# Latent attention of a two-layer diffusion trunk: value products and modulation steps issued as blocks, softmax normalised on the output

## The chip, the cores and the metric

The kernel runs on one core of a Trainium2 chip. The metric is the device time of one execution in microseconds (us); lower is better. The engines are TensorE (PE, with its weight loads shown apart as PEld), VectorE (DVE), ScalarE (ACT), GpSimd (POOL) and SyncE (SP, which here only issues transfers). About 0.2% (3.7 us here) is what a measurement of this kernel can tell from no change.

## What is computed

Two layers of a trunk over 512 latent and 256 context tokens (width 1024), each with three parallel head groups, an output projection and an MLP. The change is in the latent attention (8 heads, value width 64) and in the modulation vectors:

```
def _modulation(cond, w_mod, b_mod):
    m = jax.nn.silu(cond) @ w_mod + b_mod
    return jnp.split(m[:, None, :], 6, axis=-1)

def block(qi):                       # one block of 128 queries, all 8 heads
    s = jnp.einsum('bhqd,bhkd->bhqk', qi, kall).astype(F32) * scale
    return jnp.einsum('bhqk,bhkd->bhqd', jax.nn.softmax(s, axis=-1).astype(vall.dtype), vall)
```

Latent queries read all 768 keys. Context queries read the 256 context keys, and are needed in layer 0 alone.

## The kernel before

The program is written with tiles and a scheduler: the order in which an engine's instructions are written is a priority, and the scheduler may let a later instruction of an engine pass an earlier one that it holds to be late. Each engine then runs its queue strictly in the order so made.

`mla_attend` works in groups of two heads (`hp`) by 256 queries, and a group has four units (2 heads x 2 blocks of 128 queries). Layer 0 has 12 groups (8 that read 768 keys, 4 that read 256) and 48 units; layer 1 has 8 groups of 768 keys and 32 units. Per unit:

- `scores`: three products in split precision over the keys into a PSUM tile `mm` (L131 to L133; six instructions for 768 keys, three for 256), then `softmax_rows`: the row maximum on DVE (L425, scaled at L427), the exponential with its row sum on ACT (L430, tile `msb`, sum in `msm`), the reciprocal of the sum (L433, `mrc`) and the division of the whole row on DVE (L438).
- two turns later `values`: PE turns the row block by block (L1000, six or two instructions), ACT copies the result to `mpt` (L1001).
- four turns later, once for a group, `output`: 12 (or 4) value products into a PSUM tile `b` (L1013), alternately for head 0 and head 1. Each uses half of the PE array's columns (`tile_position=(0, 64 * z)`), so head 0 and head 1 lie side by side. `split` then writes the high part on ACT (L136) and the low part on DVE (L137).

`heads_in` turns queries and keys of the next two heads (L960). Beside this, layer 0 weaves in two `modulation` vectors: for each of 8 slices of 128 inputs four products that use a quarter of the array's columns each (L150, 32 columns, weights `wm` from memory), and `modulation_rows`, which does the same for a third vector by DVE products (L191). Layer 1 weaves in half of the output projection instead (`out_first`, L1054). After the attention comes the output projection (L1346). Value products and modulation products are plain fp32: one such product is two records in the trace. PSUM gives three buffers to `mm` and two to `b`.

In the trace layer 0's attention lies from about 363.4 us to 510.2 us of the span, layer 1's from 1329.2 us to 1445.7 us.

Of the kernel before, what the change touches and what calls it, by code (L numbers as in the profile page):

```python
# [15 lines left out]
AF = mybir.ActivationFunctionType  # L16
# [8 lines left out]
KD = 8  # L25
# [15 lines left out]
@with_exitstack  # L41
def kernel(ctx, tc, A, dbg=None, stop=None):
    nc = tc.nc
    pe, act, dve, pool, sp = nc.tensor, nc.scalar, nc.vector, nc.gpsimd, nc.sync

    class Stop(Exception):
        pass
# [17 lines left out]
    def psum_banks(mm):  # L65

        ps.stack.close()
        ps.mm, ps.b = mm, 8 - 2 * mm
        ps.n += 1
        ps.pool = ps.stack.enter_context(tc.tile_pool(name=f"ps{ps.n}", bufs=1, space=PSUM, reuse_waits="tile"))  # L70
# [5 lines left out]
    class Pool:  # L76
        def __init__(self, name, side="left"):
            opened.append(self)
            self.st = ExitStack()
            self.p = self.st.enter_context(  # L80
                tc.tile_pool(name=name, bufs=1, side=side, reuse_waits="tile"))
            self.n = 0
# [16 lines left out]
    def b_tile():  # L99
        npsum[0] += 1  # L100
        return ps.pool.tile([128, 512], F32, tag="b", name=f"b{npsum[0]}", bufs=ps.b)

    ident = persist.tile([128, 128], F32, name="ident")
# [8 lines left out]
    qrs = persist.tile([128, 6, 8], F32, name="qrs")  # L112
    cnd = persist.tile([128, KD, 2], F32, name="cnd")
    sp.dma_start(cnd, A["cond"])
    cst = persist.tile([128, KD, 32], F32, name="cst")
# [19 lines left out]
    def split(hi, lo, src):  # L135
        act.activation(hi, src, AF.Copy)  # L136
        dve.tensor_sub(lo, src, r32(hi))  # L137


    def mod_weights(l, v, k, p, bufs):  # L140
        w = p([128, 1024], tag="wm", bufs=bufs)
        sp.dma_start(w, A["w_mod"][l, k * 128:(k + 1) * 128, v * 1024:(v + 1) * 1024])
        return w

    def modulation(l, v, p, bufs=3, ws=None):
        out = b_tile()
        for k in range(KD):
            w = ws[k] if ws else mod_weights(l, v, k, p, bufs)
            for j in range(4):
                pe.matmul(out[32 * j:32 * j + 32, 0:256], cst[:, k, :], w[:, j * 256:(j + 1) * 256],  # L150
                          start=(k == 0), stop=(k == KD - 1), tile_position=(0, 32 * j))
            if k % 2:
                yield
        row = p([128, 256], tag="wr")
        act.activation(row, out[:, 0:256], AF.Copy)
        tr = b_tile()
        for c in range(2):
            pe.transpose(tr[:, c * 128:(c + 1) * 128], row[:, c * 128:(c + 1) * 128], ident)
        trv = tr[:, 0:256].rearrange("p (c j z) -> p j c z", c=2, j=4)
        bm = cols[:, l, C_BMOD + v * 8:C_BMOD + v * 8 + 8].rearrange("p (j c) -> p j c", j=4)  # L160
        for s in range(2):
            dve.tensor_add(mods[:, l, v, :, s].rearrange("p (j c) -> p j c", j=4), trv[:, :, :, s], bm)
        if v % 3 == 1:
            gain(l, v // 3)
        yield
# [252 lines left out]
                                    w[:, :, off:off + 32].rearrange("p r (g c) -> p g r c", g=4))  # L418
        return nb

    def softmax_rows(p, sb, n, nh, tag, scale=None, src=None):

        src = sb if src is None else src
        mx = p([128, nh], tag=tag + "mx", bufs=3)
        dve.tensor_reduce(mx, src, AX.X, ALU.max, negate=True)  # L425
        if scale is not None:
            dve.tensor_mul(mx, mx, scale)  # L427
        sm = p([128, nh], tag=tag + "sm", bufs=3)
        for h in range(nh):
            act.activation(sb[:, h, :n], src[:, h, :n], AF.Exp, bias=mx[:, h:h + 1], scale=1.0 if scale is None else scale[:, h:h + 1],  # L430
                           accum_out=sm[:, h:h + 1])
        rc = p([128, nh], tag=tag + "rc", bufs=3)
        dve.reciprocal(rc, sm)  # L433
        for h in range(nh):
            if h % 2:
                act.activation(sb[:, h, :n], sb[:, h, :n], AF.Copy, scale=rc[:, h:h + 1])
            else:
                dve.tensor_scalar(sb[:, h, :n], sb[:, h, :n], rc[:, h:h + 1], None, ALU.mult)  # L438
# [496 lines left out]
    def mla_attend(l, qrs, qk0, qkd, vd, mh, ml, p):  # L935
# [5 lines left out]
        v = load(p, None, [128, 6, 512], vd)  # L941
# [29 lines left out]
        groups = [(hp, q0, kr_) for hp in range(4)  # L971
                  for q0, kr_ in ((0, full), (256, full)) + (() if last else ((512, ctx_only),))]
        units = [(g, hh, qt) for g in range(len(groups)) for hh in range(2) for qt in range(2)]
        PT, SB = {}, {}

        def scores(u):
            g, hh, qt = units[u]
            hp, q0, kr_ = groups[g]
            qq, kk = T[2 * hp + hh]
            k0 = kr_[0][0]  # L980
            t = mm_tile()
            qs = slice(q0 + qt * 128, q0 + (qt + 1) * 128)
            for a, b in kr_:
                mm3(t[:, a - k0:b - k0], [x[:, qs] for x in qq], [x[:, a:b] for x in kk], True, True)
            nk = NT - k0
            SB[u] = p([128, 1, NT], tag="msb", bufs=MB)
            i, h = q0 // 128 + qt, 2 * hp + hh
            softmax_rows(p, SB[u], nk, 1, "m", qrs[:, i, h:h + 1], t[:, :nk].unsqueeze(1))

        def values(u):  # L990
            g, hh, qt = units[u]
# [12 lines left out]
        def output(u):  # L1004
            g, hh, qt = units[u]
            hp, q0, kr_ = groups[g]
            k0 = kr_[0][0]
            nkt = (NT - k0) // 128
            o = b_tile()
            for c in range(nkt):  # L1010
                for z in range(2):
                    h = 2 * hp + z
                    pe.matmul(o[64 * z:64 * z + 64, 0:256], v[:, k0 // 128 + c, h * 64:(h + 1) * 64],  # L1013
                              PT[g, z][:, c, :], start=(c == 0), stop=(c == nkt - 1), tile_position=(0, 64 * z))
            split(mh[:, hp, q0:q0 + 256], ml[:, hp, q0:q0 + 256], o[:, 0:256])

        n = len(units)
        per = n // 4
# [3 lines left out]
        for u in range(n + LO):  # L1022
# [6 lines left out]
            hp, w = divmod(u, per)  # L1029
# [157 lines left out]
    rb = next(rstd)  # L1187
    wmp.close()
    hp_ = Pool("h0")
    hh, hl = hp_([128, KD, NT], F32R), hp_([128, KD, NT], F32R)  # L1190
# [11 lines left out]
    for l in range(DEPTH):  # L1202
# [4 lines left out]
        if l:  # L1207
            fill = iter(())
            hp_ = Pool(f"h{l}")
            hh, hl = hp_([128, KD, NT], F32R), hp_([128, KD, NT], F32R)  # L1210
# [6 lines left out]
        if l:  # L1217
            squares, sums = mla_in(l, uh, ul, cqh, cql, ssq, sc, fill, late)
# [81 lines left out]
        mh2, ml2 = m2([128, 4, nt], F32R), m2([128, 4, nt], F32R)  # L1300
        sc = Pool(f"ma{l}")
        psum_banks(3)
        if last:
            xp = Pool(f"x{l + 1}", "right")
            xT, acc = xp([128, KD, nt]), xp([128, nt])
            sp.dma_start(xT, xd)
            weave((mla_attend(l, qrs, qk0, qkd[l], vd[l], mh2, ml2, sc), 1.0),
                  (out_first(l, xT, mh, ml, streams), OF))
        else:
            wmp = Pool("wm_rest")  # L1310
            weave((mla_attend(l, qrs, qk0, qkd[l], vd[l], mh2, ml2, sc), 1.0),
                  (chain(*[modulation(0, v, wmp) for v in (2, 4)]), 0.2),
                  (modulation_rows([(0, 3)], cond_rows(wmp), wmp), 0.2))
            wmp.close()
        sc.close()
        tap(f"mixb{l}", mh2); tap(f"mixbl{l}", ml2)
        tap(f"mixa{l}", mh); tap(f"mixal{l}", ml)
# [13 lines left out]
        for m in range(KD):  # L1331
            ks = range(8)
            if last:
# [3 lines left out]
                w = [x[:, m % 2 * 512:] for x in w2]  # L1337
# [200 lines left out]
```

## Time and profile before

| | |
|---|---|
| time, median of 3 runs | 1833.13 us (1832.9 to 1833.24) |
| the profiled execution: time, span | 1833.48 us, 1831.7 us |
| PE busy, of the span | 1752.5 us (96%) |
| DVE busy | 1233.4 us (67%) |
| ACT busy | 754.7 us (41%) |
| mean granted TensorE clock | 0.981 of full speed |

The span is that of the profiled execution, and its time is 1.78 us more. Busy PE counts matmuls whose ends are modelled, and they overlap: how long a piece of work holds PE is read from the start of its first instruction to the start of the next piece.

### The profile page before, as it was taken

How to read it: one execution, taken by the hardware profiler on the slowest of the kernel's cores; microseconds unless marked ns; L12 is line 12 of the kernel's file. 1: busy time of each engine (PE TensorE's matmuls, PEld its weight loads, DVE VectorE, ACT ScalarE, POOL GpSimd, SP SyncE). 2: the span in 40 equal slices, each digit the busy share in tenths (PEclk: the TensorE clock that was granted, in tenths of full speed). 3: DMA queues.
4: the chain of work that ended last, by engine and by line, in shares of the span. 5: the costliest groups of instructions: out<-in, count | busy, mean ns of one | idle time of the engine just before them, and what ended most of it. 6: DMA issues, size and time to landing. Idle time of an engine off the chain costs nothing. (4 is left out here: it accounts for less than half of the span.)

```text
span 1831.7 us, 27057 instructions
## 1 busy us (share of the span) xinstructions
PE 1752.5 (96%) x10794; PEld 1499.4 (82%) x10794; DVE 1233.4 (67%) x2247; ACT 754.7 (41%) x1262; POOL 135.8 (7%) x177
## 2 busy tenths in 40 slices
PE   5999977889999999999999999999999999999999
PEld 2788976756788888888888888888777799999997
DVE  5867777787768877767665447787877665555554
ACT  3624326566734412213212224745666653333331
POOL 1134222200000000000000000231200000000000
PEclk8999989989999999999999999999999999999999
DMA  9225423263153333333332222362041022333232
GB/s 344 72 86 167 148 70 108 82 214 113 53 198 115 138 120 134 117 137 115 130 124 60 67 68 95 114 226 81 24 167 41 31 93 94 97 99 93 93 93 81
DMA packets 73389, 206.11 MB, mean 113 GB/s; under 512 B 12556, under 2 KB 24605, under 8 KB 71856
## 3 DMA queue, kind: packets, MB, share of 16 engines
q1 hardware_dynamic: 71664, 199.15, 32.3%
q0 software_dynamic: 1600, 5.24, 0.8%
q8 instruction: 85, 1.39, 0.3%
q14 instruction: 40, 0.33, 0.1%
HBM read 182.35 MB, written 21.23 MB: 111 GB/s over the span
## 5 line engine op out<-in xcount | busy, mean ns | idle before, releaser
L273 PE MATMUL mm<-t,wh 128*128 128x512 f32 (+1 forms) x2496 | 492.5, 317 | 1.9 <-DVE t L1037 1.3
L136 ACT ACTIVATE wh<-wr 128x1024 fp32r<-128x1024 f32 (+2 forms) x176 | 185.2, 1054 | 599.4 <-PE mm L273 541.4
L273 PEld LDWEIGHTS mm<-t,wh 128*128 128x128 f32 x2496 | 371.4, 189 | 37.9 <-issue 1.9
L273 PE MATMUL mm<-t,wl 128*128 128x512 f32 (+1 forms) x1248 | 296.9, 316 | 0.0
L137 DVE TENSOR_TENSOR wl<-wr,wh 128x1024 fp32r<-128x1024 f32 (+2 forms) x176 | 214.1, 1217 | 30.5 <-ACT wh L136 27.1
L273 PE MATMUL mm<-al,wh 128*128 128x512 f32 (+1 forms) x768 | 233.6, 359 | 0.0
L273 PE MATMUL mm<-ah,wl 128*128 128x512 f32 (+1 forms) x768 | 232.2, 356 | 0.0
L1037 DVE SCALAR_TENSOR_TENSOR t<-mm,mods,t 128x512 f32<-128x512 f32 x216 | 136.3, 659 | 140.6 <-PE mm L273 132.7
L273 PE MATMUL mm<-ah,wh 128*128 128x512 f32 (+1 forms) x768 | 230.9, 354 | 0.0
L273 PEld LDWEIGHTS mm<-t,wl 128*128 128x128 f32 x1248 | 193.6, 189 | 16.2 <-DVE wl L137 0.2
L273 PEld LDWEIGHTS mm<-ah,wl 128*128 128x128 f32 x768 | 127.6, 188 | 22.5
L273 PEld LDWEIGHTS mm<-ah,wh 128*128 128x128 f32 x768 | 126.7, 188 | 23.6
L273 PEld LDWEIGHTS mm<-al,wh 128*128 128x128 f32 x768 | 126.3, 188 | 20.1
L191 DVE SCALAR_TENSOR_TENSOR wmp<-wm,t 128x1024 f32<-128x1024 f32 x64 | 78.3, 1224 | 68.3 <-DMA wm<-in_w_modr_dram 68.3
L425 DVE TENSOR_REDUCE mmx<-mm 128x1 f32<-128x768 f32 (+1 forms) x80 | 67.5, 846 | 24.9 <-PE mm L133 24.2
L136 ACT ACTIVATE ah<-relu 128x768 fp32r<-128x768 f32 (+1 forms) x64 | 47.3, 739 | 87.2 <-DVE relu L1100 87.1
L430 ACT ACTIVATE msb<-mm,mmx,qrs 128x768 f32<-128x768 f32 (+1 forms) x80 | 72.2, 904 | 24.8 <-DVE mmx L427 21.1
L1090 DVE TENSOR_SCALAR bb<-mm,cols 128x2 f32<-128x2 f32 x64 | 14.0, 219 | 97.6 <-PE mm L273 97.4
L191 DVE SCALAR_TENSOR_TENSOR wm<-wm,t 128x1024 f32<-128x1024 f32 x64 | 78.1, 1220 | 0.2
L1001 ACT ACTIVATE mpt<-mm 128x768 f32<-128x768 f32 (+1 forms) x80 | 57.6, 725 | 49.9 <-PE mm L1000 49.8
L137 DVE TENSOR_TENSOR al<-relu,ah 128x768 fp32r<-128x768 f32 (+1 forms) x64 | 52.6, 823 | 36.2 <-ACT ah L136 36.1
L1346 PE MATMUL mm<-t,wh 128*128 128x512 f32 x320 | 76.2, 352 | 0.0
(304 smaller groups left out, 2922.0 us busy)
## 6 DMA issues: line engine op xcount, KB each, us to landing
wr<-in_w_ff_dram SPq DMA_DIRECT2D x128, 512.0 KB, 3.6
wm<-in_w_modr_dram SPq DMA_DIRECT2D x64, 512.0 KB, 4.5
wm<-in_w_mod_dram SPq DMA_DIRECT2D x32, 512.0 KB, 8.4
wr<-in_w_in_t_dram SPq DMA_DIRECT2D x18, 512.0 KB, 4.0
qk<-qk_spill SPq DMA_DIRECT2D x9, 576.0 KB, 5.5
qk_spill<-upk SPq DMA_DIRECT2D x12, 384.0 KB, 2.9
kx<-kk POOLq DMA_DIRECT2D x16, 256.0 KB, 2.5
wr<-in_w_in_qk_dram SPq DMA_DIRECT2D x8, 512.0 KB, 4.6
```

The source lines that it names most:

```text
L136: act.activation(hi, src, AF.Copy)
L137: dve.tensor_sub(lo, src, r32(hi))
L191: dve.scalar_tensor_tensor(w if s else junk, w, 1.0, cr[:, s], ALU.mult, ALU.mult, accum_out=mods[:, l, v, k, s:s + 1])
L273: pe.matmul(out_[:, po:po + b - a], wk[wx], mk[mx][:, a:b], start=(k == 0 and i == 0), stop=(k == nk - 1 and i == 2))
L425: dve.tensor_reduce(mx, src, AX.X, ALU.max, negate=True)
L430: act.activation(sb[:, h, :n], src[:, h, :n], AF.Exp, bias=mx[:, h:h + 1], scale=1.0 if scale is None else scale[:, h:h + 1], accum_out=sm ...
L1001: act.activation(pt[:, 0:nkt, qt * 128:(qt + 1) * 128], tt[:, :nkt * 128].rearrange("p (c q) -> p c q", q=128), AF.Copy)
L1037: dve.scalar_tensor_tensor(xT[:, m, a:b], t[:, a:b], mods[:, l, v, m, s:s + 1], xT[:, m, a:b], ALU.mult, ALU.add)
L1090: dve.tensor_scalar(bb, t[:, 768:770], cols[:, l, C_BF1 + f:C_BF1 + f + 1], None, ALU.add)
L1346: pe.matmul(t[:, a:b], ws[wx], half[mx][:, k % 4, a:b], start=(k == ks[0] and i == 0), stop=(k == 7 and i == 2))
```

## The change

Three things. First, a wrapper round PE's `matmul` and `transpose` that is on in the attention stage alone: matmuls inside a `with pe:` block follow each other on PE with nothing between, everything written before the block stays ahead of it, and everything written after stays behind it. The value products of a group are one such block, and so are the eight modulation products of two slices. Second, the row's division is gone: the sums of a group are kept (`msm`, 2 blocks x 2 heads), and their reciprocal is spread over 128 partitions x 256 (each head's 64 value columns). Third, PE turns that reciprocal (two 128x128 transposes into the unused half of the group's `b` tile), ACT copies it back, and DVE multiplies the group's output by it before `split`.

```diff
+    class Ordered:
+        def after(self, ins, prev):
+            tc.add_manual_dep(ins, prev.name, mybir.DependencyInfo(
+                mybir.DependencyClass.NoSync, mybir.DependencyReason.DATA))
+        def issue(self, r):
+            ins = r.ins
+            if self.on:
+                for prev in self.since if self.inside else []:
+                    self.after(ins, prev)
+                if self.last is not None:
+                    self.after(ins, self.last)
+                if self.inside:
+                    self.since, self.last = [], ins
+                else:
+                    self.since.append(ins)
+            return r
...
     def modulation(l, v, p, bufs=3, ws=None):
-        out = b_tile()
+        out, wk = b_tile(), []
         for k in range(KD):
-            w = ws[k] if ws else mod_weights(l, v, k, p, bufs)
-            for j in range(4):
-                pe.matmul(out[32 * j:32 * j + 32, 0:256], cst[:, k, :], w[:, j * 256:(j + 1) * 256],
-                          start=(k == 0), stop=(k == KD - 1), tile_position=(0, 32 * j))
+            wk.append(ws[k] if ws else mod_weights(l, v, k, p, bufs))
             if k % 2:
+                with pe:
+                    for i in (k - 1, k):
+                        for j in range(4):
+                            pe.matmul(out[32 * j:32 * j + 32, 0:256], cst[:, i, :], wk[i][:, j * 256:(j + 1) * 256],
+                                      start=(i == 0), stop=(i == KD - 1), tile_position=(0, 32 * j))
                 yield
...
-        sm = p([128, nh], tag=tag + "sm", bufs=3)
+        sm = p([128, nh], tag=tag + "sm", bufs=3) if sums is None else sums
         for h in range(nh):
             act.activation(sb[:, h, :n], src[:, h, :n], AF.Exp, ..., accum_out=sm[:, h:h + 1])
+        if sums is not None:
+            return
         rc = p([128, nh], tag=tag + "rc", bufs=3)
...
-            o = b_tile()
-            for c in range(nkt):
-                for z in range(2):
-                    h = 2 * hp + z
-                    pe.matmul(o[64 * z:64 * z + 64, 0:256], v[:, k0 // 128 + c, h * 64:(h + 1) * 64],
-                              PT[g, z][:, c, :], start=(c == 0), stop=(c == nkt - 1), tile_position=(0, 64 * z))
-            split(mh[:, hp, q0:q0 + 256], ml[:, hp, q0:q0 + 256], o[:, 0:256])
+            o, rs = b_tile(), p([128, 2, 128], tag="mrc")
+            rb = rs.rearrange("p t d -> p (t d)")
+            dve.reciprocal(rs.rearrange("p t (z d) -> p t z d", z=2), SM.pop(g).unsqueeze(3).to_broadcast([128, 2, 2, 64]))
+            for t_ in range(2):
+                pe.transpose(o[:, 256 + 128 * t_:384 + 128 * t_], rs[:, t_], ident)
+            act.activation(rb, o[:, 256:512], AF.Copy)
+            with pe:
+                for c in range(nkt):
+                    for z in range(2):
+                        h = 2 * hp + z
+                        pe.matmul(o[64 * z:64 * z + 64, 0:256], v[:, k0 // 128 + c, h * 64:(h + 1) * 64],
+                                  PT[g, z][:, c, :], start=(c == 0), stop=(c == nkt - 1), tile_position=(0, 64 * z))
+            dve.tensor_mul(rb, o[:, 0:256], rb)
+            split(mh[:, hp, q0:q0 + 256], ml[:, hp, q0:q0 + 256], rb)
```

The tile `mrc` has one buffer: it holds the reciprocal, then its turned copy, then the divided output, and the next group's reciprocal is written into it.

The first place is PE's queue in layer 0 of the kernel before, a stretch of some 4 us in the middle of the stage: rows on `b_4117` are value products of one group, `ident,msb` turns a unit's row, and rows on `kh`, `kl` are one unit's scores.

```order
L1013 MATMUL b_4117<-mpt_3970,t_3494 64x256
L1000 MATMUL mm_4093<-ident,msb_4034 128x128 x6
L1013 MATMUL b_4117<-mpt_4043,t_3494 64x256
L1013 MATMUL b_4117<-mpt_3970,t_3494 64x256
L131 MATMUL mm_4101<-kh_3826,qh_3824 128x512
L132 MATMUL mm_4101<-kl_3827,qh_3824 128x512
L133 MATMUL mm_4101<-kh_3826,ql_3825 128x512
L131 MATMUL mm_4101<-kh_3826,qh_3824 128x256
L132 MATMUL mm_4101<-kl_3827,qh_3824 128x256
L133 MATMUL mm_4101<-kh_3826,ql_3825 128x256
L1013 MATMUL b_4117<-mpt_4043,t_3494 64x256
L1000 MATMUL mm_4132<-ident,msb_4059 128x128 x6
```

Value products of one group stand alone or in a few between other work here, and a product for head 1 (`mpt_4043`) is not always next to one for head 0 (`mpt_3970`).

The second place is the same group on PE's queue in the changed kernel (its products are on `b_4060`, after those of the group before, on `b_3964`); L72 and L69 are the wrapper's transpose and matmul, and `mrc` is the reciprocal.

```order
L69 MATMUL b_3964<-mpt_3893,t_3494 64x256
L72 MATMUL mm_3977<-ident,msb_3905 128x128 x6
...
L72 MATMUL mm_3999<-ident,msb_3921 128x128 x6
...
L72 MATMUL mm_4019<-ident,msb_3959 128x128 x6
L72 MATMUL b_4060<-ident,mrc_4061 128x128 x2
...
L69 MATMUL mm_4048<-kh_3795,ql_3794 128x256
L69 MATMUL b_4060<-mpt_3926,t_3494 64x256
L69 MATMUL b_4060<-mpt_3998,t_3494 64x256
L69 MATMUL b_4060<-mpt_3926,t_3494 64x256
```

Between the last product of one group and the two turns of the next group's reciprocal stand three turned rows and (in the left-out lines) two sets of scores; the group's 12 products then follow each other.

The third place is DVE's queue at that same point, before:

```order
L433 RECIPROCAL mrc_3967<-msm_3965 128x1
L427 TENSOR_TENSOR mmx_4004<-mmx_4004,qrs 128x1
L191 SCALAR_TENSOR_TENSOR wm_4152,mods<-wm_4152,t_3488 128x1024
L438 TENSOR_SCALAR msb_3961<-msb_3961,mrc_3967 128x768
L433 RECIPROCAL mrc_4009<-msm_4007 128x1
L425 TENSOR_REDUCE mmx_4035<-mm_4027 128x1
```

and in the changed kernel, where L1067 multiplies a group's output, L176 is the low part of `split`, L1056 the reciprocal, L466 and L468 the row maximum and its scaling, and L232 a modulation product:

```order
L466 TENSOR_REDUCE mmx_3960<-mm_3952 128x1
L468 TENSOR_TENSOR mmx_3960<-mmx_3960,qrs 128x1
L1067 TENSOR_TENSOR mrc_3965<-b_3964,mrc_3965 128x256
L176 TENSOR_TENSOR t_3477<-mrc_3965,t_3476 128x256
L1056 RECIPROCAL mrc_4061<-msm_3880 128x256
L466 TENSOR_REDUCE mmx_3994<-mm_3986 128x1
```

The two instructions for each unit are gone, and the reciprocal of the next group stands right behind the low part of the group before it, whose tile it takes over.

## Rows read from the trace of the kernel before

**Rows 1.** The page's first line.

```profile
span 1831.7 us, 27057 instructions
```

**Rows 2.** Busy time by stretch: us from the start, length, each engine's busy time (instructions).

```profile
core 0: us, PE busy (x) PEld busy (x) DVE busy (x) ACT busy (x) POOL busy (x), PEclk, DMA share, GB/s
...
363.40:437.00 73.60, 64.10 (x419) 45.21 (x420) 59.56 (x134) 47.31 (x81) 0.00 (x0) 0.93 0.53 187
437.00:510.20 73.20, 71.25 (x501) 48.76 (x499) 49.39 (x130) 48.65 (x99) 0.00 (x0) 1.00 0.30 103
510.20:1329.20 819.00, 802.70 (x4728) 703.81 (x4727) 572.77 (x985) 292.88 (x466) 44.37 (x60) 0.99 0.33 112
1329.20:1445.70 116.50, 115.72 (x760) 90.72 (x756) 83.57 (x167) 76.85 (x126) 0.00 (x0) 1.00 0.23 85
```

**Rows 3.** PE's waits in layer 0's attention: in all, times, longest (us).

```profile
PE mm L1000 <- ACT msb L430: 3.9, 1, 3.9
PE mm L1000 <- DVE msb L438: 2.4, 2, 2.1
```

**Rows 4.** PE's timeline in layer 0 (start, us, records): turned row, two products, scores.

```profile
461.26 0.28 PE L133 MATMUL mm<-kh,ql 96*128 96x256 f32 x1
461.39 0.88 PE L1000 MATMUL mm<-ident,msb 128*128 128x128 f32 x6
462.20 0.65 PE L1013 MATMUL b<-mpt,t 128*64 128x256 f32 x4
462.78 0.50 PE L131 MATMUL mm<-kh,qh 96*128 96x512 f32 x1
...
464.03 2.37 PE L1013 MATMUL b<-mpt,t 128*64 128x256 f32 x18
```

**Rows 5.** The same of layer 1: a whole block of 12, one product alone.

```profile
1398.49 0.28 PE L133 MATMUL mm<-kh,ql 96*128 96x256 f32 x1
1398.70 2.81 PE L1013 MATMUL b<-mpt,t 128*64 128x256 f32 x24
1401.45 0.87 PE L1000 MATMUL mm<-ident,msb 128*128 128x128 f32 x6
1402.08 0.71 PE L1054 MATMUL b<-t,wh 128*128 128x512 f32 x2
...
1422.45 0.65 PE L1013 MATMUL b<-mpt,t 128*64 128x256 f32 x2
1423.02 0.50 PE L131 MATMUL mm<-kh,qh 96*128 96x512 f32 x1
...
1439.29 2.18 PE L1000 MATMUL mm<-ident,msb 128*128 128x128 f32 x18
```

**Rows 6.** PE's timeline in layer 0: seven modulation products (14 records).

```profile
500.17 1.06 PE L150 MATMUL b<-wm,cst 128*32 128x256 f32 x14
501.16 0.38 PE L131 MATMUL mm<-kh,qh 96*128 96x256 f32 x1
```

**Rows 7.** DVE's groups by form, layer 0's attention: busy us, mean ns | idle before, releaser.

```profile
L425 DVE TENSOR_REDUCE mmx<-mm 128x1 f32<-128x768 f32 x32 | 30.4, 954 | 13.2 <-PE mm L133 12.9
L438 DVE TENSOR_SCALAR msb<-msb,mrc 128x768 f32<-128x768 f32 x32 | 19.6, 615 | 0.2
...
L433 DVE RECIPROCAL mrc<-msm 128x1 f32<-128x1 f32 x48 | 7.6, 158 | 9.8 <-ACT msb L430 9.3
...
L438 DVE TENSOR_SCALAR msb<-msb,mrc 128x256 f32<-128x256 f32 x16 | 5.5, 351 | 0.2
L137 DVE TENSOR_TENSOR t<-b,t 128x256 fp32r<-128x256 f32 x11 | 4.6, 423 | 3.4 <-ACT t L136 3.3
```

**Rows 8.** Reciprocals of one and two columns: ns min/median/max.

```profile
L433 DVE RECIPROCAL mrc<-msm x80: 150/160/167, 375.0 to 1439.0; 128x1 f32<-128x1 f32 x80
L374 DVE RECIPROCAL rnc<-rnt x6: 166/166/167, 47.3 to 141.8; 128x2 f32<-128x2 f32 x6
```

**Rows 9.** ACT's groups by form, layer 0's attention: copies of 128x256.

```profile
L136 ACT ACTIVATE t<-b 128x256 fp32r<-128x256 f32 x11 | 4.2, 385 | 8.3 <-PE b L1013 8.3
```

More of the change, by code (lines that the diff above doesn't have):

```diff
@@ L43, with __init__, matmul, transpose @@
     nc = tc.nc
-    pe, act, dve, pool, sp = nc.tensor, nc.scalar, nc.vector, nc.gpsimd, nc.sync
+    act, dve, pool, sp = nc.scalar, nc.vector, nc.gpsimd, nc.sync
+    class Ordered:
+        def __init__(self):
+            self.on, self.inside, self.last, self.since = False, False, None, []
+        def after(self, ins, prev):
[13 more added lines that the diff above has]
+            return r
+        def matmul(self, *a, **k):
+            return self.issue(nc.tensor.matmul(*a, **k))
+        def transpose(self, *a, **k):
+            return self.issue(nc.tensor.transpose(*a, **k))
+        def order(self, on):
+            self.on, self.last, self.since = on, None, []
+        def __enter__(self):
+            self.inside = True
+        def __exit__(self, *_):
+            self.inside = False
+    pe = Ordered()
     class Stop(Exception):
@@ L419, in na_bias, with softmax_rows @@
         return nb
-    def softmax_rows(p, sb, n, nh, tag, scale=None, src=None):
+    def softmax_rows(p, sb, n, nh, tag, scale=None, src=None, sums=None):
         src = sb if src is None else src
@@ L973, in mla_attend @@
         units = [(g, hh, qt) for g in range(len(groups)) for hh in range(2) for qt in range(2)]
-        PT, SB = {}, {}
+        PT, SB, SM = {}, {}, {}
         def scores(u):
@@ L978, in scores @@
             hp, q0, kr_ = groups[g]
+            if hh == qt == 0:
+                SM[g] = p([128, 2, 2], tag="msm", bufs=3)
             qq, kk = T[2 * hp + hh]
@@ L987, in scores @@
             i, h = q0 // 128 + qt, 2 * hp + hh
-            softmax_rows(p, SB[u], nk, 1, "m", qrs[:, i, h:h + 1], t[:, :nk].unsqueeze(1))
+            softmax_rows(p, SB[u], nk, 1, "m", qrs[:, i, h:h + 1], t[:, :nk].unsqueeze(1), SM[g][:, qt, hh:hh + 1])
         def values(u):
@@ L1302 @@
         psum_banks(3)
+        pe.order(True)
         if last:
@@ L1314 @@
             wmp.close()
+        pe.order(False)
         sc.close()
```

## Prediction

> **What bounds the kernel now.** I read the page first and then its busy time by stretch. The span is 1831.7 us [rows 1] and the profiled time 1833.48 us, so 1.78 us lie around the span; the median of the runs shown is 1833.13 us, 0.35 us below the profiled run. By stretch [rows 2] PE is busy 64.1 of 73.6 us in the first half of layer 0's attention, 71.25 of 73.2 us in its second half, 115.72 of 116.5 us in layer 1's, and 802.7 of 819 us between the two stages. So from 437 us on PE is what the time follows, and what PE does not have to do there comes off the time. In the first half PE waits: most of it twice, 3.9 us and 2.1 us, for a unit's softmax [rows 3]. DVE is the next engine: 59.56 of 73.6 us in that half, far less elsewhere.
>
> **What a column block costs PE.** The reader should look at starts, not at busy times. One value product alone (2 records) holds PE from 1422.45 to 1423.02, 0.57 us [rows 5]. Two products, one for each head, hold it from 462.20 to 462.78, 0.58 us [rows 4]. A whole block of 12 (24 records) takes 1398.70 to 1401.45, 2.75 us [rows 5]. So the unit is a *pair*: 0.43 us each ((2.75 - 0.58) / 5), plus about 0.15 us once for every run of such products, and a product without its partner costs as much as the pair. Seven modulation products take 500.17 to 501.16, 0.99 us [rows 6]: two sets of four at 0.42 us and the same 0.15 us.
>
> Beside that a run costs something at its edge: from the last score instruction to a turned row 0.13 us pass (461.26 to 461.39 [rows 4]), to a value product 0.21 us (1398.49 to 1398.70 [rows 5]); six turns take 0.63 us when other work follows (1401.45 to 1402.08 [rows 5]) and 0.81 us when products follow (461.39 to 462.20 [rows 4]). So an entry costs 0.08 us after scores, 0.18 us after turns.
>
> **What the blocks save.** I counted runs and pairs in the two built orders.
>
> - Layer 0, value products: 112 products stand in 36 runs that fill 68 pairs; after, 12 runs and 56 pairs. 36 x 0.15 + 68 x 0.43 = 34.6 us become 12 x 0.15 + 56 x 0.43 = 25.9 us: -8.7 us.
> - Layer 0, modulation: 64 products in 19 runs and 21 sets become 8 runs and 16 sets: 19 x 0.15 + 21 x 0.42 = 11.7 us become 7.9 us: -3.8 us.
> - Layer 0, entries: 27 after scores become 8, 14 after turns become 10: 19 x 0.08 + 4 x 0.18 = -2.2 us.
> - Layer 1, value products: 96 products in 14 runs and 53 pairs become 8 runs and 48 pairs: 24.9 us become 21.8 us: -3.1 us; entries after scores 7 to 3: -0.3 us. Layer 1 was nearly blocked before.
>
> **What is added on PE.** Two turns for each group, 24 and 16. Eighteen turns in a row hold PE 2.18 us [rows 5], 0.12 us each: +2.9 us and +1.9 us. PE's sum is -11.8 us in layer 0 and -1.5 us in layer 1, -13.3 us.
>
> **Off PE's path.** In layer 0 DVE loses 19.6 + 5.5 us of divisions and 7.6 us of small reciprocals [rows 7], and gets 12 reciprocals of 128x256 and 12 products of that size out of PSUM; the latter I take like the low part, 0.42 us [rows 7]. No row shows a wide reciprocal. The low bound is a simple operation of that size, 0.35 us (the division of 256 columns [rows 7]). The high bound is the slope of the reciprocals themselves: 160 ns for one column, 166 ns for two [rows 8], some 7 ns (6 to 7) a column, so 0.16 + 255 x 0.007 = 1.94 us. I take 1.9 us, since those rows are the same operation. DVE then changes by 12 x (1.9 + 0.42) - 32.7 = -4.9 us (with the low bound -23.5 us). ACT gets 12 and 8 copies of 128x256 at 0.385 us [rows 9], 7.7 us in all, under 47.31 and 48.65 us of work in halves of 73 us and 76.85 us in 116.5 us [rows 2]: hidden while PE has work in its queue, and behind the chain below where it has not.
>
> The Trainium skill (VectorE: DVE Perf Modes, First, the fixed hardware budget) says that the reciprocal is an iterative divide with a repeat count of 8. With the clock of 0.96 GHz under Specifications there, an estimate for 256 columns is 256 x 8 / 0.96, about 2.1 us. No row of this kernel shows it; with it in place of 1.9 us the chain below is 0.2 us longer in each hand-over between groups, and the sum would be 1 to 2 us worse.
>
> **The first waits.** A row is now turned as soon as its exponential ends: 0.615 + 0.158 = 0.77 us earlier [rows 7]. The two exposed waits of 3.9 and 2.1 us [rows 3] shrink by that each, -1.5 us; what is late next there is the exponential itself. The later waits of layer 0 are short, and layer 1 starts with projection products to fill them; I count nothing there.
>
> **A new chain between groups.** The tile `mrc` has one buffer. So after a group's last product come, in this order, the output's multiplication (0.42 us), the high part on ACT (0.385 us), the low part on DVE (0.42 us), the next group's reciprocal (1.9 us), and only then can PE turn it: 3.1 us plus hand-overs. PE's queue is in order, so if the turns come up earlier, the scores, turned rows and products behind them wait too. How long PE has until then I summed from the new order with the prices above: at the place shown, three turned rows at about 0.6 us and two sets of scores at 1.2 us (462.78 to 464.03 less the entry [rows 4]), 4.2 us. Of 18 hand-overs ten have 4.9 to 13.9 us, and eight (five in layer 0, three in layer 1) have 3.3 to 4.4 us. Those eight have no room for one instruction that stands ahead in DVE's queue (a row maximum takes 0.954 us [rows 7]). The reciprocal also stands ahead of the next row maximum, which then comes 1.9 us later. I charge the eight 0.6 us each: +5 us. Bounds: nothing with the cheap reciprocal; 8 x 1.6 us = 13 us if two such instructions are always ahead.
>
> **The ends.** After the last group the multiplication makes the chain to the output projection 0.42 us longer. The projection takes its input slices in order and needs that group's heads as the last of each, so it starts on work that is ready: hidden, and 0.4 us if not. The modulation weights are now needed for two slices at a time; eight such steps share layer 0's two stretches of 73 us [rows 2], some 18 us for each, in which their transfers land. A late one would hold PE at its block with everything behind it; I count nothing.
>
> **The sum.** -13.3 - 1.5 + 5 = -9.8 us from 1833.48 us gives 1823.7 us for such an execution, 1823.3 us as a median: **1823 us**.
>
> **Rivals.**
>
> *No new wait, 1818 us.* If a wide reciprocal costs like a simple operation (0.35 us), the chain is 1.6 us and all 18 hand-overs have room: -14.8 us from 1833.1 us, 1818 us; a little less if the half-speed stretches at layer 0's start shrink as well (PEclk 0.93 in the first half [rows 2]). For it: 6 ns between two rows of 160 and 166 ns is a thin slope, and the spread of one form is 17 ns. Against: nothing else there names a cheap one. Chance 0.2.
>
> *Layer 0 follows DVE, 1829 us.* In the first half DVE is busy 59.56 of 73.6 us with PE waiting for it [rows 2, 3]. DVE keeps nearly all its work there when the reciprocal is 1.9 us. If that half does not get shorter at all, about half of layer 0's 11.8 us is lost: 1833.1 - 13.3 + 5.9 - 1.5 + 5 = 1829 us. Against: there PE waited for single chains, not for a full queue. Chance 0.2.
>
> *Slower: the hand-overs stall, 1838 us.* The mechanism of the eight tight groups in all 18: the reciprocal waits for the fourth exponential and the tile, DVE's modulation products stand between, and PE stands at two turns with everything behind them. It decides at a stall of 14.8 / 18, about 0.8 us for each group; 1.1 us for each gives 1838 us. Against: ten have room of 4.9 us and more. Chance 0.07.
>
> *The blocks give nothing.* If pairs in one long block cost as much as pairs in short runs, the entries and the 0.15 us of a run stay, and only the missing pairs and sets count, 17 x 0.43 + 5 x 0.42 = 9.4 us against 4.8 us of turns: 1833.1 - 9.4 + 4.8 - 1.5 + 5 = 1832 us. But the whole block of 12 is already in the trace at 2.75 us. Chance 0.03.
>
> **Numbers.** The forecast with its own bounds (stalls of 0 to 9 us) is 1818 to 1828 us, chance 0.5. With the cheap reciprocal below and DVE's pace above, 1815 to 1831 us leaves out the stalled case and the tails. Against a band of 3.7 us (below 1829.4 us is faster, above 1836.8 us is slower): faster 0.49 + 0.2 + 0.1 = 0.79; same 0.14; slower 0.07.
>
> **What would show it.** In the changed profile: value products in 20 groups of 24 or 8 records with 2.74 and 1.01 us from start to next start; a row RECIPROCAL of 128x256 at 1.9 us; 40 more turns; layer 0's stretch about 136.5 us (146.8 - 11.8 - 1.5 + 3), layer 1's about 117 us (116.5 - 1.5 + 1.8); PE waits on `mrc` of about 5 us in all, at the groups with little work between blocks. The prediction is wrong if PE's waits in layer 0 grow by more than 10 us, or if the reciprocal is under 0.5 us and they still grow.

## The result and the profile after

The changed kernel takes 1849.68 us (median of 4 runs, 1843.11 to 1852.97) beside 1833.02 us of the kernel before: ratio 1.0087, interval 1.0063 to 1.011. Run once more in another session, it takes 1846.02 us (8 runs) beside 1837.26 us (25 runs of the kernel before, 1832.72 to 1843.68): 1.0053, interval 1.0033 to 1.0073. It is slower, by 9 to 17 us, where 10 us less was forecast. (A ratio is taken over all runs of both kernels, so it need not be that of the medians.)

The profiled execution takes 1849.73 us with a span of 1848 us, against [rows 1]. Its busy time by stretch (columns as in [rows 2]): up to the attention of layer 0, that attention, the work between, the attention of layer 1.

```profile
0.00:368.10 368.10, 320.58 (x1986) 265.79 (x1986) 256.41 (x541) 161.16 (x335) 91.36 (x117) 0.96 0.38 131
368.10:523.70 155.60, 132.99 (x960) 98.64 (x960) 105.49 (x189) 99.62 (x191) 0.00 (x0) 0.96 0.40 146
523.70:1340.10 816.40, 801.09 (x4710) 702.92 (x4709) 572.90 (x985) 292.69 (x466) 44.29 (x60) 0.99 0.33 111
1340.10:1461.90 121.80, 115.94 (x774) 91.90 (x772) 78.61 (x120) 79.18 (x134) 0.00 (x0) 1.00 0.23 81
```

Layer 0's attention is 155.6 us long with PE busy for 133 us of it: PE stands still for 22.6 us, where it did for 11.4 us before. Layer 1's grew from 116.5 to 121.8 us with PE's busy time almost the same (115.72 and 115.94 us).

One trap is in the first row. The first stage starts at 368.1 us instead of 363.4 us, though PE's order up to there is the same. That part is not the change's: in the 14 profiles of this study (13 kernels, the changed one twice) the first turn of `qk` starts anywhere from 362.7 to 372.2 us. One place where it differs is early: the same modulation records in the kernel before and, in the second pair of rows, in the changed kernel (PE's timeline):

```profile
36.56 1.93 PE L150 MATMUL b<-wm,cst 128*32 128x256 f32 x32
...
39.58 0.64 PE L150 MATMUL b<-wm,cst 128*32 128x256 f32 x8
```
```profile
38.45 3.64 PE L69 MATMUL b<-wm,cst 128*32 128x256 f32 x32
...
43.27 0.64 PE L69 MATMUL b<-wm,cst 128*32 128x256 f32 x8
```

Each of the 32 records takes nearly twice as long in the changed kernel, as at the lower of PE's two clock levels (1.2 for 2.4 GHz); the eight a little later take the same time in both. The granted clock is given as 1.00 for both places, but in the changed kernel that is no reading: its trace has no clock entry before 43.2 us. In the three profiles whose first stage starts latest (368.2, 369.7 and 372.2 us) the first entry, at the upper level, comes at 43.2, 49.4 and 50.6 us; in the other eleven PE is at the upper level from 34.2 to 35.9 us on. So a late rise of the clock goes with a late start; what delays it the runs do not show. Since this lies ahead of all that the change touches, I read each kernel by stage as well: **L0**, from layer 0's first turn of `qk` to one fixed matmul of the output projection behind it (169.2 us before), and **L1**, the same for layer 1, up to one fixed matmul of the work behind its projection (139.4 us). By these the changed kernel loses 5.6 us in L0 and 5.3 us in L1 in the first profile, 4.8 and 5.4 us in the second; the rest of the first run's 16 us is 4.7 us ahead of the stages and 0.7 us between them.

PE's waits in layer 0 and then in layer 1 (in all, times, longest), which answer to [rows 3]:

```profile
PE mm L69 <- ACT mpt L1046: 5.5, 9, 0.9
PE mm L72 <- DVE ql L1007: 5.1, 4, 1.6
PE mm L72 <- ACT msb L471: 4.7, 4, 3.5
PE b L69 <- ACT mrc L1060: 2.7, 4, 0.8
PE mm L69 <- DVE ql L1007: 1.8, 2, 1.1
PE mm L72 <- ACT mpt L1046: 0.7, 3, 0.2
...
PE b L69 <- ACT mrc L1060: 2.9, 4, 1.3
PE mm L69 <- ACT mpt L1046: 1.4, 2, 0.7
```

The largest are waits for a buffer `mm`: scores (L69) that can't start before ACT has copied an earlier turned row out (`mpt`), turns (L72) that can't start before DVE has written the low part of a head (`ql`). The waits of `b` are a group's first product, which waits for ACT's copy of the turned reciprocal.

The same kinds of wait for a buffer `mm` in layer 0 of the kernel before:

```profile
PE mm L1000 <- DVE ql L964: 1.8, 1, 1.8
PE mm L960 <- DVE ql L964: 0.7, 1, 0.7
...
PE mm L960 <- ACT mpt L1001: 0.2, 1, 0.2
```

So the waits for `mpt` rose from 0.2 to 6.2 us and those for `ql` from 2.5 to 6.9 us, while those of a turned row for its softmax fell from 6.3 us ([rows 3]) to 4.7 us.

PE's timeline shows one of each: in layer 0 (first four rows), and in layer 1.

```profile
454.79 0.82 PE L72 MATMUL mm<-ident,msb 128*128 128x128 f32 x6
455.44 0.38 PE L72 MATMUL b<-ident,mrc 128*128 128x128 f32 x2
456.51 0.50 PE L69 MATMUL mm<-kh,qh 96*128 96x512 f32 x1 [0.68 <-ACT mpt L1046]
...
457.75 1.08 PE L69 MATMUL b<-mpt,t 128*64 128x256 f32 x8
...
1380.15 0.38 PE L72 MATMUL b<-ident,mrc 128*128 128x128 f32 x2
1381.07 2.81 PE L69 MATMUL b<-mpt,t 128*64 128x256 f32 x24 [0.53 <-ACT mrc L1060]
1383.81 0.87 PE L72 MATMUL mm<-ident,msb 128*128 128x128 f32 x6
```

Compare [rows 4]: there two value products stand between a turned row and the next scores, and no wait. Here the products of the group whose reciprocal was just turned come as a block only after those scores, and PE waits 0.68 us for the buffer.

DVE's and ACT's new instructions in layer 0, by form (as in [rows 7, 9]):

```profile
L1056 DVE RECIPROCAL mrc<-msm 128x256 f32<-128x256 f32 x12 | 20.9, 1745 | 0.6 <-ACT msb L471 0.5
...
L1067 DVE TENSOR_TENSOR mrc<-b,mrc 128x256 f32<-128x256 f32 x11 | 4.7, 423 | 17.8 <-PE b L69 17.7
```
```profile
L1060 ACT ACTIVATE mrc<-b 128x256 f32<-128x256 f32 x12 | 4.6, 380 | 3.8 <-PE b L72 3.8
```

### The profile page after: what moved, and what is told of

Read it like the earlier page. It is cut to its first block, busy times and chain, and to the rows that moved or that the text cites. A ratio compares the mean times of both kernels' runs of the same rounds, so it can differ in the third digit from the quotient of the medians.

```text
span 1848.0 us, 27007 instructions
## 1 busy us (share of the span) xinstructions
PE 1752.9 (95%) x10834; PEld 1505.5 (81%) x10834; DVE 1225.4 (66%) x2127; ACT 760.5 (41%) x1282; POOL 135.6 (7%) x177
## 5 line engine op out<-in xcount | busy, mean ns | idle before, releaser
L69 PE MATMUL mm<-t,wh 128*128 128x258 f32 (+2 forms) x2816 | 570.0, 322 | 1.8 <-DVE t L176 0.6
L69 PEld LDWEIGHTS mm<-t,wh 128*128 128x128 f32 x2816 | 423.2, 189 | 47.6 <-issue 2.3
L69 PE MATMUL mm<-t,wl 128*128 128x258 f32 (+2 forms) x1408 | 342.7, 320 | 0.0
L69 PEld LDWEIGHTS mm<-t,wl 128*128 128x128 f32 x1408 | 219.0, 189 | 20.4 <-issue 0.4
L69 PE MATMUL mm<-al,wh 128*128 128x512 f32 (+1 forms) x768 | 233.8, 359 | 0.0
L69 PE MATMUL mm<-ah,wl 128*128 128x512 f32 (+1 forms) x768 | 232.4, 356 | 0.0
L176 DVE TENSOR_TENSOR wl<-wr,wh 128x1024 fp32r<-128x1024 f32 (+2 forms) x176 | 213.9, 1216 | 26.9 <-ACT wh L175 23.6
L69 PE MATMUL mm<-ah,wh 128*128 128x512 f32 (+1 forms) x768 | 231.0, 354 | 0.0
L69 PEld LDWEIGHTS mm<-ah,wh 128*128 128x128 f32 x768 | 126.8, 188 | 23.5
L69 PEld LDWEIGHTS mm<-ah,wl 128*128 128x128 f32 x768 | 127.7, 188 | 22.4
L69 PEld LDWEIGHTS mm<-al,wh 128*128 128x128 f32 x768 | 126.3, 188 | 20.0
L232 DVE SCALAR_TENSOR_TENSOR wmp<-wm,t 128x1024 f32<-128x1024 f32 x64 | 78.3, 1223 | 69.4 <-DMA wm<-in_w_modr_dram 67.3
L69 PE MATMUL b<-wh,t 128*128 128x256 f32 (+1 forms) x416 | 94.3, 309 | 4.6 <-ACT hu L658 3.9
L466 DVE TENSOR_REDUCE mmx<-mm 128x1 f32<-128x768 f32 (+1 forms) x80 | 66.8, 841 | 32.4 <-PE mm L69 31.0
L69 PEld LDWEIGHTS b<-wh,t 128*128 128x128 f32 x416 | 73.3, 205 | 6.4 <-ACT hu L658 4.3
L232 DVE SCALAR_TENSOR_TENSOR wm<-wm,t 128x1024 f32<-128x1024 f32 x64 | 78.0, 1218 | 0.1
```

What stands on the lines that cost most here:

```text
L69: return self.issue(nc.tensor.matmul(*a, **k))
L232: dve.scalar_tensor_tensor(w if s else junk, w, 1.0, cr[:, s], ALU.mult, ALU.mult, accum_out=mods[:, l, v, k, s:s + 1])
```

## The experiments

Two words first. A *barrier* is either side of a block: what is written before it stays ahead on PE, what is written after stays behind. *Fill* is small work that PE does while its next larger work waits for something.

Times of one session are read against the kernel before in that session. A difference below 3.7 us cannot be told from no change by the medians; several below are that small, and for those the readings by stage decide. These come from one profile for each kernel; the two profiles of the changed kernel agree within 0.8 us in L0 and 0.1 us in L1 and in idle time. Besides L0 and L1 I worked out from PE's records, between layer 0's first turn and its last value product: how long value and modulation products hold PE (start to next start, less idle time), the same for the turns of the reciprocal, and PE's idle time (end of one record to the start of the next). "Half" is how much of L0 lay at the lower level of PE's clock, 1.2 GHz; each us there costs at most half a us, so kernels that differ in it compare better by idle time than by L0.

| kernel | median, us | before beside it | ratio | L0 | half | products | turns | idle | L1 |
|---|---|---|---|---|---|---|---|---|---|
| before | 1833.0 | | | 169.2 | 10.2 | 46.4 | | 11.4 | 139.4 |
| changed | 1849.7 | 1833.0 | 1.0087 | 174.8 | 13.7 | 36.3 | 4.3 | 22.6 | 144.7 |
| changed, again | 1846.0 | 1837.3 | 1.0053 | 174.0 | 10.2 | 35.1 | 4.3 | 22.5 | 144.8 |
| blocks alone | 1842.7 | 1838.7 | 1.0030 | 174.3 | 17.1 | 38.3 | | 23.9 | 140.9 |
| normalisation alone | 1840.2 | 1838.7 | 1.0016 | 171.2 | 10.2 | 42.3 | 4.1 | 12.0 | 142.7 |
| changed, narrow reciprocal | 1842.2 | 1838.7 | 1.0023 | 172.3 | 13.7 | 35.7 | 4.5 | 21.7 | 144.9 |
| changed, turns into `mm` | 1851.3 | 1838.7 | 1.0073 | 179.7 | 10.2 | 35.7 | 3.9 | 27.5 | 142.4 |
| value blocks alone | 1833.7 | 1837.3 | 0.9983 | 167.5 | 13.7 | 38.8 | | 17.2 | 140.6 |
| modulation blocks alone | 1832.4 | 1837.0 | 0.9975 | 165.6 | 6.8 | 41.7 | | 12.7 | 139.5 |
| blocks in thirds | 1835.4 | 1837.3 | 0.9991 | 163.5 | 6.8 | 36.7 | | 15.2 | 143.4 |
| thirds, modulation free | 1837.9 | 1837.0 | 1.0012 | 167.0 | 13.7 | 40.8 | | 13.9 | 143.2 |
| heads swapped | 1826.7 | 1837.3 | 0.9949 | 162.3 | 10.2 | 38.8 | | 12.7 | 138.1 |
| heads swapped, modulation blocks | 1829.5 | 1837.0 | 0.9966 | 164.3 | 6.8 | 36.9 | | 15.5 | 138.2 |
| heads swapped, normalisation | 1836.0 | 1837.0 | 1.0000 | 167.9 | 10.2 | 40.5 | 4.0 | 10.6 | 141.6 |

**The two halves of the change.** First the blocks with the old softmax:

```diff
-            o, rs = b_tile(), p([128, 2, 128], tag="mrc")
-            dve.reciprocal(...)
-            for t_ in range(2): pe.transpose(...)
-            act.activation(rb, o[:, 256:512], AF.Copy)
+            o = b_tile()
...
-            dve.tensor_mul(rb, o[:, 0:256], rb)
```

> The ordering wrapper and both kinds of block, with the old softmax (reciprocal of each row's sum, rows divided on DVE); nothing is turned, copied or multiplied at a group's end. Theory A (the barriers at both sides of a block take PE's freedom to fill waits): most of layer 0's 11 us of added PE waits stay, mainly scores that wait for ACT's copy to `mpt`, so my PE sum without the turns (-18 us) is largely eaten: 1825 to 1833 us. Theory B (the new chain reciprocal, turn, copy, block is what costs): the added waits go, and the time is near 1833 - 18 = 1815 us, 1812 to 1822 us. Theory C (about 4.7 us of the loss lie ahead of the first attention stage, in code whose order is unchanged, and belong to where the half-clock stretches fall, not to the change): the first stage may begin anywhere from 363 to 368 us here too.

Measured +4.0 us (interval of the ratio 1.001 to 1.0051). The waits stay without any normalisation, as in theory A: 23.9 us idle in layer 0. They eat the whole saving, more than A's 1825 to 1833 us allowed, and they are not the ones that A named: scores wait only 1.2 us for `mpt`, and the largest are those of turned rows for `ql`. As in theory C the start has its part: the first stage begins at 369.7 us, one of the three late ones. PE's waits in layer 0:

```profile
PE mm L72 <- DVE ql L1007: 8.9, 6, 2.1
PE mm L72 <- ACT msb L471: 5.8, 4, 4.5
PE mm L69 <- ACT msb L471: 3.2, 5, 0.9
PE mm L72 <- DVE mmx L468: 2.9, 3, 1.4
PE mm L69 <- ACT mpt L1044: 1.2, 3, 0.5
```

Then the normalisation with no order (the order is never switched on, modulation as before):

```diff
-        pe.order(True)
...
-        pe.order(False)
```

> The other half alone: no ordering and modulation as before; the sums' wide reciprocal, its two turns, the copy and the output's multiplication stay. Theory A: without barriers the scheduler fills the waits, so only the 4.8 us of turns less 1.5 us of the first waits remain: about 1836 us, 1833 to 1839 us. Theory B: PE still waits for the copy before a group's first product and for DVE behind 20 reciprocals of 1.75 us: 1842 to 1850 us.

Measured +1.5 us (1.0004 to 1.0029), and by stage +2.0 and +3.3 us; idle 12.0 us in layer 0, near the kernel before. The 5.3 us of the two stages are nearer to theory A (some 3 us more) than to B (9 us or more). In layer 1 the two halves' costs, +1.5 and +3.3 us, make most of the changed kernel's 5.3 us.

**Two repairs of the chain.** The narrow reciprocal:

```diff
-            dve.reciprocal(rs.rearrange("p t (z d) -> p t z d", z=2), SM.pop(g).unsqueeze(3).to_broadcast([128, 2, 2, 64]))
+            r4 = p([128, 2, 2], tag="mr4", bufs=2)
+            dve.reciprocal(r4, SM.pop(g))
+            dve.tensor_copy(rs.rearrange("p t (z d) -> p t z d", z=2), r4.unsqueeze(3).to_broadcast([128, 2, 2, 64]))
```

> The full change, but the reciprocal is taken of the four sums of a group alone (128x4) and spread to 128x256 by a copy on DVE: about 0.17 + 0.35 us in place of 1.75 us, twenty times. If the wide reciprocal makes DVE late (waits for `ql` of 5.8 us, for row maxima, and the hand-over of the one `mrc` buffer), the time falls by 4 to 10 us from 1849.7 us, to 1840 to 1846 us, and the waits for `ql` go back to some 2.5 us. If DVE's extra time lies beside PE's other waits, no change, 1847 to 1852 us.

Measured +3.5 us (1.0005 to 1.0041) where the changed kernel has +8.8 us in another session. By these medians the first branch came true; by stage it did not: L0 is about 2 us shorter, L1 not at all (the first stage also starts 2 to 5 us earlier), and the waits of turns for `ql` did not fall (5.1 us with the wide one):

```profile
PE mm L72 <- DVE ql L1007: 8.4, 6, 1.5
```

So by stage the wide reciprocal costs about 2 us, and not by way of `ql`.

The turns into the last quarter of a turned row's `mm` tile:

```diff
+            gt = g if u == n - 1 else g - 1 if (hh, qt) == (0, 0) else -1
+            if gt >= 0:
+                for t_ in range(2):
+                    pe.transpose(tt[:, 768 + 128 * t_:896 + 128 * t_], RS[gt][:, t_], ident)
+                act.activation(RS[gt].rearrange("p t d -> p (t d)"), tt[:, 768:1024], AF.Copy)
```

> The full change, but the reciprocal is turned into the unused last quarter of a turned row's `mm` tile (the one of the next group's first unit, issued right behind that row), so the block's own `b` tile is not read by ACT before the block. If the 5.7 us of waits of value products for ACT's copy come from sharing that tile, they vanish, about 5 us less: 1843 to 1846 us. If the wait only moves (the copy holds an `mm` buffer longer, and the scores wait for it), 1848 to 1852 us.

Measured +12.6 us (1.0051 to 1.0095). No product waits for the copy any more, and layer 1 gains 2.3 us. In the changed kernel no data goes from the copy to the products, so the wait was the shared tile's (this kernel also turns the reciprocal a turn of the loop earlier). But layer 0 loses 5 us: the copy now holds an `mm` buffer, and turns and scores wait. The wait moved. PE's waits in layer 0:

```profile
PE mm L72 <- ACT mpt L1046: 6.9, 11, 1.5
PE mm L72 <- DVE ql L1007: 6.0, 4, 2.1
```

**The changed kernel again**, beside the next three.

> The changed kernel unaltered, on the chip and beside the runs of the three kernels that follow, since the kernel before reads 1832.5 to 1833.2 us in one session and 1831.9 to 1844.1 us in another. If the 16 us are the change's own, 1849 us or more here and over 14 us above the kernel before. If some 5 us of them were the place of the half-clock stretches ahead of the first attention stage, the difference is 9 to 13 us, with layer 0's stage about 5.6 us and layer 1's about 5.3 us longer than in the kernel before, as in the first profile.

Measured +8.8 us: below the 9 to 13 us by a hair, with the two stages as in the first profile.

**Which blocks make PE wait.** Value blocks alone, modulation issued as before and outside the order:

```diff
-                with pe:
-                    for i in (k - 1, k):
...
+            for j in range(4):
+                nc.tensor.matmul(out[32 * j:32 * j + 32, 0:256], cst[:, k, :], w[:, j * 256:(j + 1) * 256],
```

> Old softmax; the order is on, but only the value products are blocks: modulation products are issued as before, outside the order, so the scheduler may place them anywhere. Theory A1 (value products were what PE did while all three `mm` buffers were held, so gathering them costs the waits): layer 0 idles 20 us or more, as with both kinds of block (23.9 us), and the time is within 2 us of that kernel. Theory A2 (the modulation blocks, each a barrier that waits for two weights, are the cost): layer 0's idle time falls to 12 to 15 us and the time by 6 us or more, to about 1833 to 1836 us.

Measured -3.5 us (0.9968 to 0.9997). Idle 17.2 us lies between the two theories, the time in A2's range: both kinds of block idle PE. The other way round, modulation blocks alone, with the group's products outside the order:

```diff
-            with pe:
...
-                    pe.matmul(o[64 * z:64 * z + 64, 0:256], ...
+                    nc.tensor.matmul(o[64 * z:64 * z + 64, 0:256], ...
```

> Old softmax; only the modulation steps are blocks with their barriers, and the value products are issued outside the order, as in the kernel before. Both kinds of block idle 23.9 us in layer 0, value blocks alone 17.2 us, the kernel before 11.4 us. If the two kinds add up, modulation blocks alone idle about 11.4 + 6.7 = 18 us and save 3.7 us of PE work: layer 0's stage about 172 us by the ends that gave 169.2 us before, layer 1 as before (139.4 us), 1835 to 1839 us. If value blocks are what makes the modulation barriers wait, the idle time stays below 14 us and the time falls by 1 to 4 us.

Measured -4.6 us (0.9957 to 0.9993), idle 12.7 us. The costs do not add: modulation blocks idle PE by 1.3 us when value products are free and by 6.7 us (23.9 less 17.2) when these are blocks too. I read that as: what a barrier costs depends on what else PE may issue meanwhile.

**Is it the fill, or the barriers?** Three blocks of four products in three turns of the loop:

```diff
-            with pe:
-                for c in range(nkt):
+            for b in range(0, nkt, 2):
+                with pe:
+                    for c in (b, b + 1):
...
+                if b + 2 < nkt:
+                    yield
...
```

> Old softmax and the order with both kinds of block, but a group's 12 value products are three blocks of four (two slices, both heads), one in each of three turns of the loop. PE pays 24 more entries and runs in layer 0 at 0.15 to 0.25 us, about +5 us, and 15 in layer 1, about +3 us. Theory A1 (fill): PE has four products to issue in three places in place of twelve in one, and the idle time of layer 0 falls from 23.9 us by 8 us or more, so the time is equal to that of whole blocks or better. Barriers as such: with 24 more of them the idle time stays or grows, and the time is 6 to 10 us worse.

Measured -1.8 us (0.9973 to 1.0009). Layer 0 has 16 more blocks and layer 1 too (not 24 and 15: a group of 256 keys stays one block). With them layer 0 idles 8.7 us less than with whole blocks, so it is where the products stand, not the number of barriers. No kernel here gathers every group's products into one run without barriers, so what a barrier adds to the gathering is not shown apart. Layer 1, which had little idle time to fill, pays for the extra runs (143.4 us against 140.9 us). With modulation free besides:

> Old softmax; a group's value products as three blocks of four in the order, modulation outside it, as in the kernel before. If the wait is fill that the blocks gather (value blocks in thirds) plus modulation's barriers, layer 0 idles 10 to 13 us, as with the swapped heads (12.7 us), and the stage takes 161 to 164 us; layer 1 stays near the 143.4 us of thirds, since nothing changes there. About 1829 to 1834 us. If thirds with modulation inside the order had most of the gain already, within 2 us of that kernel (1835.4 us, against 1837.3 us of the kernel before beside it).

Measured +0.9 us (0.9997 to 1.0027): a miss. Idle fell by 1.3 us only, while modulation, free again, holds PE for 11.4 us in place of 8.0 us, which the expected 161 to 164 us left out. L0 is 167.0 us, with twice as much of it at the lower clock (13.7 us for 6.8 us, 3.4 us at most); its first stage also starts latest of all, at 372.2 us. Thirds inside the order had most of the gain.

**Gathering without an order.** The kernel before with one line changed:

```diff
-                for z in range(2):
+                for z in (1, 0):
```

> The kernel before with one line changed: the two heads of each slice are written in the order (1, 0), so that the product of the head whose turned row comes last is written first. No order, no blocks, old softmax. In the built order the value products then stand in 20 runs and 58 pairs of layer 0 (36 and 68 before) and 11 runs and 49 pairs of layer 1 (14 and 53): by my prices 27.9 us for 34.6 us and 22.7 us for 24.9 us, -8.9 us. If PE keeps its fill, the waits stay near 11 us in layer 0 and the time falls by 6 to 10 us against the kernel before. If the gain of any gathering is lost in waits, within 2 us of it.

Measured -10.6 us (0.993 to 0.9967), 19.4 us below the changed kernel in the same session: faster than both. By stage that is 8.2 us. The product that becomes ready last is written first, so its partner is ready when it goes, and the scheduler keeps its freedom. PE's longest waits in layer 0 stay as in [rows 3] (12.7 us idle, 11.4 us before):

```profile
PE mm L1000 <- ACT msb L430: 3.9, 1, 3.9
PE mm L1000 <- DVE msb L438: 2.3, 1, 2.3
PE mm L131 <- ACT msb L430: 1.8, 3, 0.9
```

and its timeline in layer 0 shows products both gathered (eight in the first row) and as fill (one pair between turns and scores):

```profile
470.93 1.95 PE L1013 MATMUL b<-mpt,t 128*64 128x256 f32 x16
472.81 0.44 PE L1000 MATMUL mm<-ident,msb 128*128 128x128 f32 x2
473.17 0.65 PE L1013 MATMUL b<-mpt,t 128*64 128x256 f32 x4
473.75 0.39 PE L131 MATMUL mm<-kh,qh 96*128 96x256 f32 x1
```

Two additions to it. Modulation blocks:

> Old softmax; modulation steps as blocks with their barriers, value products outside the order with the heads of each slice written in the order (1, 0). In the built order the value products of layer 0 stand in 23 runs and 59 pairs, those of layer 1 in 11 and 49. If the two gains add (value products stay free to fill the waits, so modulation's barriers cost little): layer 0's stage 165.6 us (modulation blocks alone) less 5 us or more, 159 to 161 us, layer 1's 138 us, the time 1822 to 1826 us, 11 to 15 us below the kernel before. If the gathered value products are no fill for modulation's barriers, layer 0 idles 17 us or more and the time is 1828 to 1832 us, no better than the swap alone (10.6 us below).

Measured -7.5 us (0.9954 to 0.9979), no better than the swap alone: idle 15.5 us, short of the 17 us named but more than with single products (12.7 us): gathered products fill modulation's barriers less well. And the deferred normalisation without an order:

> The deferred normalisation (wide reciprocal, two turns, copy, output's product) without any order, with the heads of each slice written in the order (1, 0). Against the kernel with the swap alone, the normalisation adds the turns' 4.3 + 2 us, some waits for ACT's copy, and takes 1.5 us from the first waits: layer 0 about 166 us (162.3 us with the swap alone), layer 1 about 142 us (138.1 us), 1833 us or some 6 to 8 us above the swap alone. If the normalisation was only bad behind barriers, within 3 us of the swap alone.

Measured 1836.0 us (ratio 0.9988 to 1.0012), 9.3 us above the swap alone in another session, more than the 6 to 8 us expected; by stage 5.6 and 3.5 us. The value products hold PE for 28.0 us of layer 0 in both, so about 9 us is the normalisation's price without any barrier; 1.7 us of it are modulation products, which the scheduler's order leaves in 19 runs here and in 14 with the swap alone. Alone, on the kernel before, it showed less (5.3 us by stage) because the scheduler's new order also gathered products there: 30.5 us for 34.7 us.

## Why the prediction was wrong

The step that failed is the sentence of the first part, "what PE does not have to do there comes off the time". The sum has two entries for waits, -1.5 us for the first waits and +5 us for the new chain, and none for waits that the scattered products had covered; that missing term measured about 10 us in layer 0. The prediction's own sign of being wrong came: PE's waits in layer 0 grew by more than 10 us (11.2 us).

- *What the blocks save: right, but for the entries.* In layer 0 the value products were forecast to go from 34.6 to 25.9 us; they measure 34.7 and 28.3 us, where one block starts in a stretch of granted clock 0.50 (442.6 to 449.4 us) and takes 5.08 us in place of 2.75 us; 27.1 us in the second profile. Modulation: 11.7 to 7.9 us forecast, 11.7 to 8.0 us measured. Layer 1: 24.9 to 21.8 us forecast, 24.9 to 21.9 us measured. The prices of pair, set and run carry. The entries (-2.2 us in layer 0) do not show: scores and turned rows hold PE for 76.4 us of L0 before and 76.4 us in the second profile of the changed kernel, both with 10.2 us at the lower clock.
- *The waits: wrong.* PE's idle time rose from 11.4 to 22.6 us in layer 0 and from 0.8 to 5.9 us in layer 1. The first waits shrank as forecast (6.3 to 4.7 us); the waits for an `mm` buffer, `mpt` and `ql` together, rose from 2.7 to 13.1 us in layer 0. Value and modulation products need no `mm` buffer; standing singly they were what PE did while ACT and DVE emptied the three `mm` buffers. I priced the scattered products as waste. A run of them costs 0.15 us more than the same products in a block; without it PE now waits up to 0.9 us for a copy to `mpt` and up to 1.6 us for `ql`. That blocks do this without the normalisation is shown (23.9 us idle), and that products spread over more places take 8.7 us of it back (thirds). The busy shares on which the sentence stood, 71.25 of 73.2 us and 115.72 of 116.5 us [rows 2], are those of a PE with that fill in it.
- *The new chain: right in size by luck, wrong place.* I expected PE to stand at the turns, waiting for the reciprocal in `mrc`'s one buffer, 5 us in all. No such wait of PE's matmuls is in the trace. The wait stands one step on: the block shares the tile `b` with the turned reciprocal and waits for ACT's copy of it, 2.7 and 2.9 us. Putting the turns elsewhere removed it.
- *The turns: under-sized.* 2.9 and 1.9 us were forecast; 24 and 16 turns hold PE 4.3 and 2.9 us, since they stand in pairs, not in a row of 18 as in [rows 5].
- *The reciprocal: 1.9 us forecast, 1.745 us measured.* The slope from two narrow rows, thin as it was, was a good guide. The Trainium skill's repeat count of 8 (VectorE: DVE Perf Modes, First, the fixed hardware budget) gave an estimate of 2.1 us; the trace has less.
- *The rivals.* Slower got 0.07, by hand-overs at `mrc`; it came by the lost fill instead, which no rival named. It should have been one: the prediction quotes the very place [rows 4] where two products stand between a turned row and the next scores, and prices it only as an entry.
- *The sum by stage.* L0: products -10.1 us, turns +4.3 us, idle time +11.2 us, against +5.6 us measured. L1: products -3.0 us, turns +2.9 us, idle time +5.1 us, against +5.3 us.

The first stage starts up to 9 us later in some profiles, and in the three latest the clock rises late; why it does was not tried, and stays open. Between the two profiles of the changed kernel the start makes 2.8 of 3.4 us. How much of the difference between 16.7 us in one session and 8.8 us in the other is due to it is not shown: the kernel before read 4.2 us more in the second session, where it has no profile.

## What to carry to other kernels

An engine that is 97% busy or more can be so because a scheduler fills its waits with small work; before gathering that work, ask for each place where it stands what the engine would wait for there without it. Gather by making partners ready together (write the late one first) rather than by a barrier that holds everything else. And when a step is moved off one engine, look for the tile it shares with its consumer: a wait can sit in the tile rather than in the data.

## What the runs showed of the hardware

A reciprocal of 128x256 on DVE takes 1.745 us: with 160 ns for one column [rows 8], (1745 - 160) / 255 = 6.2 ns for each further column, where the division of 256 columns takes 351 ns in all [rows 7]. And one program's runs may agree within 0.7 us in one session (1832.51 to 1833.24) and spread over 12 us in the next (1831.92 to 1844.14): for a difference below 1%, compare stages as well as medians.
